# Max-pool and subtract: tiles of six rows in four slots in place of four rows in six

## The chip, the cores and the metric

The kernel runs on one core of one Trainium2 chip. The metric is the device time in microseconds (us) of one execution, as the median of several.

## The reference

```python
B, C, H, W = 8, 64, 256, 256          # float32
x_r = x.reshape(B, C, 32, 8, 32, 8)
pooled = x_r.max(axis=(3, 5))         # maximum of each 8 x 8 window
upsampled = np.repeat(np.repeat(pooled, 8, axis=2), 8, axis=3)
return x - upsampled
```

Every 8 x 8 window of each image has its own maximum subtracted. The input is 134.22 MB, the output as much.

## The kernel before

Eight image lines of one channel, 8 x 256 = 2048 floats or 8 KB, hold 32 whole windows. The kernel calls this a row (`ROW`). There are 16384 rows, or 128 for each of the 128 partitions, and a row in all partitions together is 1.049 MB. A tile is a number of rows per partition: partition p of a tile takes neighbouring rows of DRAM, so that each partition's share is one contiguous piece, 32 KB for a tile of four rows.

The tiles are listed in `sizes`: a first tile of four rows, 30 tiles of four rows (`ROUNDS * SLOTS`), and a last one of four. The first is loaded and stored as two halves of two rows (`HEAD`), the last is loaded whole, and computed and stored in parts of two, one and one row (`TAIL`). The data lie in one SBUF buffer, `ring`, of `SLOTS * SIZE` = 24 rows per partition. Tile i has the slot `(i - 1) % SLOTS`, the first tile the last slot. The maxima lie in `tops`. A tile is computed in place and stored from where it was loaded to.

Nothing is left to a scheduler: each engine has its list of instructions, and semaphores tie them together.

- SyncE issues all loads (L110) in the order of the tiles. Before the load of tile i it waits until the tile that had the slot before is stored (L107, semaphore `stored[slot]`).
- TensorE does no arithmetic. It waits for each load in turn and adds one to `filled` (L117, L120), so that VectorE has one semaphore to wait for.
- VectorE runs two nested loops over `ROUNDS` and `SLOTS` (L139, L140) with the head before and the tail after. For each part it takes one from `filled` (`take`, L75), and calls `pool_and_subtract`: one maximum over the windows of all rows of the part (L81), a wait for it (`reduced`), and one subtraction per row (L93), the last of which adds to `ready`.
- ScalarE waits for `ready` and issues the stores (L129), which add to `stored[slot]` or, at the end, to `final`.

Loads and stores have a DMA queue each (q1 and q10 on the page), over the same 16 DMA engines.

Of the kernel before, what the change touches and what calls it, by code (L numbers as in the profile page):

```python
# [1 line left out]

# [4 lines left out]

F32 = mybir.dt.float32
ROW = 2048


HEAD = [2, 2]
SIZE = 4
ROUNDS = 5
TAIL = [2, 1, 1]
SLOTS = 6


@with_exitstack
def kernel(  # L20
    ctx: ExitStack,
    tc: tile.TileContext,
    x: bass.AP,
    out: bass.AP,
):
    nc = tc.nc
    P = nc.NUM_PARTITIONS
    B, C, H, W = x.shape
    pH = pW = 8
    oW = W // pW  # L30

    x_rows = x.rearrange("b c (oh ph) w -> (b c oh) (ph w)", ph=pH)
    out_rows = out.rearrange("b c (oh ph) w -> (b c oh) (ph w)", ph=pH)
    sizes = [sum(HEAD)] + [SIZE] * (ROUNDS * SLOTS) + [sum(TAIL)]
    assert sum(sizes) * P == x_rows.shape[0] and max(sizes) == SIZE
    starts = [P * sum(sizes[:i]) for i in range(len(sizes))]
    last = len(sizes) - 1

    data = ctx.enter_context(tc.tile_pool(name="data", bufs=1))
    ring = data.tile([P, SLOTS * SIZE * ROW], F32, name="ring")  # L40
    tops = data.tile([P, SLOTS * SIZE * oW], F32, name="tops")
    first = [tc.alloc_semaphore(f"first{i}") for i in range(len(HEAD))]
    loaded = [tc.alloc_semaphore(f"loaded{i}") for i in range(SLOTS)]
    stored = [tc.alloc_semaphore(f"stored{i}") for i in range(SLOTS)]
    final = tc.alloc_semaphore("final")
    filled = tc.alloc_semaphore("filled")
    reduced = tc.alloc_semaphore("reduced")
    ready = tc.alloc_semaphore("ready")

    def slot_of(i):  # L50

        return (i - 1) % SLOTS

    def dram(rows, i):

        n = sizes[i]
        return rows[starts[i] : starts[i] + P * n].rearrange("(p r) d -> p (r d)", r=n)

    def sbuf(i, lo, R):
        at = (slot_of(i) * SIZE + lo) * ROW  # L60
        return ring[:, at : at + R * ROW]

    def top(i, lo, R):
        at = (slot_of(i) * SIZE + lo) * oW
        return tops[:, at : at + R * oW]

    def cuts(parts):
        lo = 0
        for R in parts:
            yield lo, R  # L70
            lo += R

    def take(sem, n):

        nc.vector.wait_ge(sem, n).then_inc(sem, -n)  # L75

    def pool_and_subtract(part, top, R):

        wins = part.rearrange("p (r ph ow pw) -> p r ph ow pw", r=R, ph=pH, ow=oW)
        maxs = top.rearrange("p (r ow) -> p r ow", r=R)  # L80
        nc.vector.tensor_reduce(  # L81
            out=maxs if R > 1 else maxs[:, 0],
            in_=(
                wins.rearrange("p r ph ow pw -> p r ow ph pw")
                if R > 1
                else wins[:, 0].rearrange("p ph ow pw -> p ow ph pw")
            ),
            axis=mybir.AxisListType.XY,
            op=mybir.AluOpType.max,
        ).then_inc(reduced, 1)  # L90
        take(reduced, 1)
        for r in range(R):
            sub = nc.vector.tensor_tensor(  # L93
                out=wins[:, r],
                in0=wins[:, r],
                in1=maxs[:, r].unsqueeze(1).unsqueeze(3).to_broadcast([P, pH, oW, pW]),
                op=mybir.AluOpType.subtract,
            )
        sub.then_inc(ready, 1)

    with tc.tile_critical(no_gpsimd_drain=True):

        landed = [0] * SLOTS
        for i in range(len(sizes)):
            slot = slot_of(i)
            if landed[slot]:
                nc.sync.wait_ge(stored[slot], 16 * landed[slot])  # L107
            for k, (lo, R) in enumerate(cuts(HEAD if i == 0 else [sizes[i]])):
                part = slice(lo * ROW, (lo + R) * ROW)
                nc.sync.dma_start(out=sbuf(i, lo, R), in_=dram(x_rows, i)[:, part]).then_inc(  # L110
                    first[k] if i == 0 else loaded[slot], 16
                )
                landed[slot] += 1


        for k in range(len(HEAD)):
            nc.tensor.wait_ge(first[k], 16).then_inc(filled, 1)  # L117
        for i in range(1, len(sizes)):
            turn = (i - 1) // SLOTS + 1
            nc.tensor.wait_ge(loaded[slot_of(i)], 16 * turn).then_inc(filled, 1)  # L120


        done = n_final = 0
        for i in range(len(sizes)):
            for lo, R in cuts(HEAD if i == 0 else TAIL if i == last else [SIZE]):
                part = slice(lo * ROW, (lo + R) * ROW)
                done += 1
                nc.scalar.wait_ge(ready, done)
                nc.scalar.dma_start(out=dram(out_rows, i)[:, part], in_=sbuf(i, lo, R)).then_inc(  # L129
                    stored[slot_of(i)] if i + SLOTS <= last else final, 16  # L130
                )
                n_final += i + SLOTS > last
        nc.scalar.wait_ge(final, 16 * n_final)


        for lo, R in cuts(HEAD):
            take(filled, 1)
            pool_and_subtract(sbuf(0, lo, R), top(0, lo, R), R)
        with nc.vector.Fori(0, ROUNDS):  # L139
            with nc.vector.Fori(0, SLOTS) as slot:  # L140
                take(filled, 1)
                pool_and_subtract(
                    ring[:, bass.ds(slot * (SIZE * ROW), SIZE * ROW)],
                    tops[:, bass.ds(slot * (SIZE * oW), SIZE * oW)],
                    SIZE,
                )
        take(filled, 1)
        for lo, R in cuts(TAIL):
            pool_and_subtract(sbuf(last, lo, R), top(last, lo, R), R)


# [1 line left out]
_INS = ['x']  # L153
_OUTS = [((8, 64, 256, 256), 'float32')]


# [23 lines left out]
```

## Time and profile before

| | |
|---|---|
| median of 3 runs | 627.47 us (627.42 to 627.5) |
| profiled execution: time | 627.26 us |
| profiled execution: span | 625.5 us |
| VectorE busy | 562.6 us (90%) |
| maximum of a part of 4 rows (L81) | 8.69 us, x30 |
| maximum of a part of 2 rows, 1 row | 4.42 us x3, 2.28 us x2 |
| subtraction of a row (L93) | 2.29 us, x128 |
| loads, stores issued | 33, 35 |
| median from issue to landing, 4 rows | load 62.1 us, store 35.9 us |
| DMA packets | 9792 |

The page divides the span into 40 equal slices and gives for each the busy share of VectorE in tenths, the share of the 16 DMA engines and what they moved. The time from issue to landing includes the time that a transfer stands in its queue behind earlier ones. A wait is named with the line that waits and what it waited for; the line L75 is the wait inside `take`. In the timeline a line has the start, the duration, the engine, the line of code, and in brackets the idle time just before.

### The profile page before, as it was taken

The page shows a single profiled execution, that of the slowest core. Times are in us where ns is not written, and L with a number is a line of the kernel's source. Part 1 is how long each engine was busy: PE and PEld are TensorE (multiplying, and loading weights), DVE is VectorE, ACT ScalarE, POOL GpSimd, SP SyncE. Part 2 cuts the span into 40 slices and gives each one's busy share as a digit, 9 for nine tenths or more (in the row PEclk, how much of TensorE's full clock was granted, in tenths as well). Part 3 has the DMA queues.
Part 4 walks back from the last instruction along what each step waited for, and adds up shares of the span by engine and source line. Part 5 has one row for each costly group of instructions (what it writes and reads, how often), then busy time and mean ns, then how long its engine had stood idle before and what let it go on. Part 6 is the DMA issues. An engine that isn't in the chain of part 4 may idle for free. (4 is left out here: it accounts for less than half of the span.)

```text
span 625.5 us, 613 instructions
## 1 busy us (share of the span) xinstructions
DVE 562.6 (90%) x163; POOL 0.2 (0%) x4
## 2 busy tenths in 40 slices
DVE  4999999998898888988889888898888998888983
POOL 0000000000000000000000000000000000000000
DMA  8999999999999999999999999999999999999998
GB/s 369 402 434 438 436 434 436 434 436 434 434 432 427 425 434 436 436 436 434 436 434 436 434 434 427 430 425 436 436 436 434 436 436 434 434 436 434 425 427 363
DMA packets 9792, 268.44 MB, mean 429 GB/s; under 512 B 1088, under 2 KB 1088, under 8 KB 1088
## 3 DMA queue, kind: packets, MB, share of 16 engines
q1 hardware_dynamic: 4752, 134.22, 49.9%
q10 hardware_dynamic: 5040, 134.22, 49.7%
HBM read 134.22 MB, written 134.22 MB: 429 GB/s over the span
## 5 line engine op out<-in xcount | busy, mean ns | idle before, releaser
L81 DVE TENSOR_REDUCE tops<-ring (+2 forms) x35 | 278.4, 7953 | 48.4 <-DVEq L75 48.4
L93 DVE TENSOR_TENSOR ring<-ring,tops (+1 forms) x128 | 285.0, 2287 | 5.2 <-DVEq L75 0.2
L164 POOL MEMSET const-bfloat16-1.0<- 128x1 bf16 x1 | 0.1, 102 | 0.0
L164 POOL MEMSET const-uint8-127<- 128x1 uint8 x1 | 0.1, 102 | 0.0
L164 POOL MEMSET const-float32-0.0<- 128x1 f32 x1 | 0.1, 99 | 0.2 <-issue 0.2
L164 POOL MEMSET const-float32-1.0<- 128x1 f32 x1 | 0.1, 99 | 0.0
## 6 DMA issues: line engine op xcount, KB each, us to landing
ring<-in_x_dram SPq DMA_DIRECT2D x31, 4096.0 KB, 62.1
out_dram<-ring ACTq DMA_DIRECT2D x30, 4096.0 KB, 35.9
out_dram<-ring ACTq DMA_DIRECT2D x3, 2048.0 KB, 19.3
ring<-in_x_dram SPq DMA_DIRECT2D x2, 2048.0 KB, 9.5
out_dram<-ring ACTq DMA_DIRECT2D x2, 1024.0 KB, 9.2
```

Source lines behind the costliest of these rows:

```text
L81: nc.vector.tensor_reduce(out=maxs if R > 1 else maxs[:, 0], in_=(wins.rearrange("p r ph ow pw -> p r ow ph pw") if R > 1 else wins[:, 0]. ...
L93: sub = nc.vector.tensor_tensor(out=wins[:, r], in0=wins[:, r], in1=maxs[:, r].unsqueeze(1).unsqueeze(3).to_broadcast([P, pH, oW, pW]), op ...
L164: nc = _bacc.Bacc("TRN2", target_bir_lowering=False, num_devices=1)
```

## The change

The 30 tiles of four rows become 20 tiles of six (`SIZE`, `TILES`), and the ring has four slots of six rows in place of six slots of four: the same 24 rows. A partition's share of such a tile is a contiguous piece of 48 KB. The first tile keeps its four rows and its halves (`HEAD` for loads and computing, `HEAD_OUT` for stores, both two and two), and lies in the last slot, of which it fills four of six rows. The last tile keeps its four rows and its parts.

VectorE's two nested loops become one loop over the tiles, with the slot worked out as `i % SLOTS` on each pass. For the head and the last tile, VectorE waits for the load's semaphore itself; TensorE passes on the loads between only. For these parts the wait between the maximum and the subtractions counts up on a semaphore of its own, `pooled`, in place of taking one from `reduced`. The load of tile i again waits for the stores of tile i - `SLOTS`, so tile 4 is the first that waits, for both stores of the head.

```diff
-HEAD = [2, 2]
-SIZE = 4
-ROUNDS = 5
+HEAD, HEAD_OUT = [2, 2], [2, 2]
+SIZE, TILES = 6, 20
 TAIL = [2, 1, 1]
-SLOTS = 6
+SLOTS = 4
...
-    sizes = [sum(HEAD)] + [SIZE] * (ROUNDS * SLOTS) + [sum(TAIL)]
+    sizes = [sum(HEAD)] + [SIZE] * TILES + [sum(TAIL)]
...
+    pooled = tc.alloc_semaphore("pooled")
...
-    def pool_and_subtract(part, top, R):
+    def pool_and_subtract(part, top, R, nth=None):
...
-        ).then_inc(reduced, 1)
-        take(reduced, 1)
+        ).then_inc(reduced if nth is None else pooled, 1)
+        if nth is None:
+            take(reduced, 1)
+        else:
+            nc.vector.wait_ge(pooled, nth)
...
-                landed[slot] += 1
+            landed[slot] += len(HEAD_OUT) if i == 0 else 1
...
-        for k in range(len(HEAD)):
-            nc.tensor.wait_ge(first[k], 16).then_inc(filled, 1)
-        for i in range(1, len(sizes)):
+        for i in range(1, last):
             turn = (i - 1) // SLOTS + 1
             nc.tensor.wait_ge(loaded[slot_of(i)], 16 * turn).then_inc(filled, 1)
...
-            for lo, R in cuts(HEAD if i == 0 else TAIL if i == last else [SIZE]):
+            for lo, R in cuts(HEAD_OUT if i == 0 else TAIL if i == last else [SIZE]):
...
-                done += 1
+                done = [sum(HEAD[: k + 1]) for k in range(len(HEAD))].index(lo + R) + 1 if i == 0 else done + 1
...
-        for lo, R in cuts(HEAD):
+        for k, (lo, R) in enumerate(cuts(HEAD)):
+            nc.vector.wait_ge(first[k], 16)
+            pool_and_subtract(sbuf(0, lo, R), top(0, lo, R), R, k + 1)
+        with nc.vector.Fori(0, TILES) as i:
+            slot = i % SLOTS
             take(filled, 1)
-            pool_and_subtract(sbuf(0, lo, R), top(0, lo, R), R)
-        with nc.vector.Fori(0, ROUNDS):
-            with nc.vector.Fori(0, SLOTS) as slot:
-                take(filled, 1)
-                pool_and_subtract(
-                    ring[:, bass.ds(slot * (SIZE * ROW), SIZE * ROW)],
-                    tops[:, bass.ds(slot * (SIZE * oW), SIZE * oW)],
-                    SIZE,
-                )
-        take(filled, 1)
-        for lo, R in cuts(TAIL):
-            pool_and_subtract(sbuf(last, lo, R), top(last, lo, R), R)
+            pool_and_subtract(
+                ring[:, bass.ds(slot * (SIZE * ROW), SIZE * ROW)],
+                tops[:, bass.ds(slot * (SIZE * oW), SIZE * oW)],
+                SIZE,
+            )
+        nc.vector.wait_ge(loaded[slot_of(last)], 16 * ((last - 1) // SLOTS + 1))
+        for k, (lo, R) in enumerate(cuts(TAIL)):
+            pool_and_subtract(sbuf(last, lo, R), top(last, lo, R), R, len(HEAD) + k + 1)
```

## The prediction

> **What bounds the kernel now.** I read the page's slices first, then its DMA packets and queues, then the waits, then the timeline.
>
> ```profile
> span 625.5 us, 613 instructions
> DVE 562.6 (90%) x163; POOL 0.2 (0%) x4
> ...
> DVE  4999999998898888988889888898888998888983
> ...
> DMA  8999999999999999999999999999999999999998
> GB/s 369 402 434 438 436 434 436 434 436 434 434 432 427 425 434 436 436 436 434 436 434 436 434 434 427 430 425 436 436 436 434 436 436 434 434 436 434 425 427 363
> DMA packets 9792, 268.44 MB, mean 429 GB/s; under 512 B 1088, under 2 KB 1088, under 8 KB 1088
> ...
> q1 hardware_dynamic: 4752, 134.22, 49.9%
> q10 hardware_dynamic: 5040, 134.22, 49.7%
> ```
>
> The reader is to see that the two queues (q1 loads, q10 stores) together occupy the 16 DMA engines for 99.6% of the span, at a flat 434 to 436 GB/s. VectorE is 90% busy, not full. The waits say which way the dependence runs:
>
> ```profile
> DVE tops L81 <- DVEq L75: 48.4, 26, 8.5
> ...
> SPq L110 <- DMA out_dram<-ring: 522.6, 26, 47.2
> ```
>
> VectorE waits 48.4 us in 26 places at its L75 wait, which is the wait for a load; SyncE spends 522.6 us waiting for stores to free a slot. Two lines of the timeline, 22 tiles apart, give the steady period:
>
> ```profile
> 152.70 8.69 DVE L81 TENSOR_REDUCE tops<-ring  x1 [1.64 <-DVEq L75]
> ...
> 578.66 8.69 DVE L81 TENSOR_REDUCE tops<-ring  x1 [1.63 <-DVEq L75]
> ...
> 613.92 2.29 DVE L93 TENSOR_TENSOR ring<-ring,tops 128x2048 f32<-128x2048 f32 x1
> ```
>
> (578.66 - 152.70) / 22 = 19.362 us per tile of four rows, with 1.63 us of idle in it. The last subtraction ends at 616.2, and the last store lands at 624.4: VectorE is done 8 us before the transfers. So the time is DMA bytes and DMA overhead, from the first packet at about 2 us to the end, and nothing else decides unless both queues run empty at once.
>
> [...] The trace has a little more: its packet records show 309, 611 and 1213 ns for packets of 8, 16 and 32 KB, each starting 3.1 to 3.9 ns before the previous one ends, so the true steps are 305.9, 607.1 and 1209.4 ns. Against 301.18 ns per 8 KB at 27.2 GB/s per engine that leaves 4.7 ns for each of the three sizes, and 5.9 ns for the small packet that signals the end. [...] In the trace, load and store packets alternate one to one in the steady part. [...] The pitch here is 32 KB and becomes 48 KB; no run here shows a loss from pitch.
>
> **The change part by part.**
>
> *Transfers.* Bytes are the same: 128 rows of 1.049 MB in and out. A transfer covers 128 partitions, so 8 packets on each of 16 engines, and one small packet each. Before there are 33 loads + 35 stores = 68 transfers: 68 x 128 = 8704 data packets and 68 x 16 = 1088 small ones, as the page counts. After there are 2 + 20 + 1 = 23 loads and 2 + 20 + 3 = 25 stores: 48. Twenty fewer transfers save on each engine 20 x 8 x 4.7 ns + 20 x 5.9 ns = 0.87 us. The period gives the same price another way: 8.389 MB at 435.2 GB/s is 19.275 us, 0.087 us below the measured 19.362; that is 0.043 us for each of the two transfers, and 20 x 0.043 = 0.87 us. This lies on the path in full, since the engines have no idle time. The bounds: the recorded durations taken at face value (1213 = a + 4b, 611 = a + 2b, so a = 9 ns) would give 160 x 9 + 20 x 9 = 1.6 us. From below: if the gain per packet vanishes, 0. I take 0.87, since steps between starts, not durations, make up the time.
>
> *VectorE.* The reduce of 1, 2, 4 rows takes 2.28, 4.42, 8.69 us, about 2.14 per row: 12.96 us for six (estimate). Six subtractions step by 2.205 us: 13.2. With 0.24 us of gaps a tile takes 26.4 us. The DMA period of a six-row tile is 12 x 8 x 0.30118 + 2 x 0.043 = 29.0 us, so VectorE still waits 2.6 us per tile. The added register operation of i % SLOTS and the removed outer loop lie in this idle time: no cost. Without that cover: a branch takes 33 ns and a semaphore wait 21 ns in the trace, so two or three more such per tile, 0.1 us, would be 2 us over 20 tiles. The head and tail waits that go straight to the load's semaphore drop a hop over TensorE's queue; all of VectorE's queue stands behind them, but it waited for the same load before. No cost. SyncE and ScalarE issue 10 fewer transfers each, 0.33 us apiece, beside waits of hundreds of us: nothing.
>
> *Slots, steady.* A slot's round is 4 x 29.0 = 116.0 us (before 6 x 19.36 = 116.2). VectorE holds it 26.4, leaving 89.6 for store and load, which need 29 each while they share: 31 us of spare backlog. Before: 116.2 - 17.7 - 2 x 19.4 = 59.8. Smaller, but not gone. And a dry load queue alone costs nothing, because stores then run at the full rate.
>
> *Start.* The head's two loads are unchanged, so VectorE starts at 8.47 again and the first store goes out at 17.57. By about 19 us some 6.9 rows are in. Tile 1 now needs 10 rows, not 8. Load packets of 48 KB alternate with head stores of 16 KB, so loads get 3/4 of the rate (3.2 us per row): tile 1 lands at about 30 us, VectorE idles 3 to 4 us from 26.4. That idle is paid from its slack. The new wait to watch: SyncE holds tile 4's load (before it was tile 6's) until both head stores landed, and all later loads queue behind it. Those stores have 4 rows at a quarter of the rate, 4 x 2.41 x 4 = 38.5 us, so they land at about 58; the 15 rows then still queued for tiles 1 to 3 last 15 x 3.2 = 48 us, to about 67. Nine us of cover; the engines don't stop.
>
> *End.* The last load (4 rows) lands about 24 us after tile 20's, as its packets alternate with larger store packets ((4 + 6) x 2.41). VectorE spends 26.4 on tile 20, then 18.3 on the tail (597.89 to 616.2 now), so it ends 20.7 us after the last load. Stores left at that load: all of tile 20 and the tail, 10 rows = 24 us, plus what tile 19 has left, some 10 us. So stores end 10 us or more after VectorE, as against 8 now. No cost.
>
> **Sum.** The profiled execution has a span of 625.5 and a time of 627.26; the change takes 0.87: 624.6 and 626.4. The median shown, 627.47, lies 0.21 above it, so I forecast 626.6. That is 0.14% less, inside the 0.2% (1.25 us) that a measurement of this kernel can about tell from no change.
>
> **The rivals.**
> (a) *The forecast*: overhead of 20 transfers goes, nothing else. For it: full engines, identical steps at three packet sizes. With 0.4 us either way for the uneven start of the engines: 626.2 to 627.0. Chance 0.62.
> (b) *Packets of 48 KB run slower*, from the pitch of 48 KB in HBM or a limit of the engine. Place: 40 transfers x 8 = 320 packets per engine, 320 x 1.812 = 580 us of the time. From 2.1 us of loss (0.87 + 1.25), 6.6 ns per packet or 0.37% of the rate, the change ends slower. At 0.5% the time is 626.6 + 2.9 = 629.5. Against it: the step per byte is constant from 8 to 32 KB[...]. For it: the trace has no 48 KB packet, and the point of decision is low. Chance 0.17, a part of it below that point.
> (c) *The transfer isn't one packet per partition.* Cut in 32 + 16 KB: 160 packets more than now per engine instead of 160 fewer, +0.75 - 0.12 = +0.63 us, 628.1, still within 0.2%. Cut in three of 16 KB: 480 more, +2.26 - 0.12 = +2.14 us, 629.6, slower. Against it: packets of 32 KB pass whole. Chance 0.07, nearly half of it slower.
> (d) *The saving is the durations' 9 ns*, 1.6 us, or one of the start's ragged packets goes too: 625.9, faster by 0.25%. Against it: the steps between packet starts. Chance 0.10.
> (e) *Both queues dry with only four slots*, at the first wait for the head stores, where the cover is 9 us: a gap of 2 us gives 628.6, slower. Chance 0.04.
>
> Faster by over 0.2% is (d) and the edge of (a): 0.14. Slower is most of (b), part of (c), and (e): 0.20. Within 0.2%: 0.66. The range 625.7 to 628.7 holds (a), (d), the mild part of (b) and (c), and (e).
>
> **What would show it.** Right: 6144 data packets and 768 small ones; six-row reduces of about 12.96 us; a steady period of 29.0 us per tile with idle of about 2.6 us before the reduce; queues together at 99.5% or more; VectorE done some 10 us before the end; span about 624.6. Wrong: a period of 29.1 or more, which is (b); more than 6912 packets, (c); a slice in the first 80 us well below 400 GB/s other than the first, (e); last subtraction within 4 us of the end, a tail that VectorE sets.

## The result, and the profile after

The changed kernel took 629.48 us as the median of 6 executions (628.4 to 631.29), beside 627.49 us before (627.36 to 627.79). The ratio is 1.0031, with a 95% interval of 1.0016 to 1.0047: slower by 0.3%, where 0.14% faster was forecast. (Ratios, here and below, are to the kernel before, and leave out executions over 1.5% above the fastest of their kernel: one each in experiments 10, 15 and 18.) The second thing to see is the spread: 2.9 us between executions of one program, where the kernel before has 0.4. The profiled execution took 629.67 us with a span of 627.9.

The page of the changed kernel, with the lines that answer to those shown of before (DMA packets count data packets and small ones; a queue's line has packets, MB, and the share of 16 engines' span):

```profile
span 627.9 us, 517 instructions
DVE 560.1 (89%) x153; POOL 0.2 (0%) x4
...
DVE  4699999999998888989898989898898989898991
...
DMA  8999999999999999999999999999999999999996
GB/s 367 434 426 428 432 448 420 435 442 423 438 438 413 442 445 410 442 448 413 442 448 410 442 451 407 445 448 410 445 448 410 445 448 407 448 448 404 458 410 286
DMA packets 6912, 268.44 MB, mean 428 GB/s; under 512 B 768, under 2 KB 768, under 8 KB 768
...
q1 hardware_dynamic: 3312, 134.22, 49.7%
q10 hardware_dynamic: 3600, 134.22, 49.4%
```

The packets are those that were counted: 6144 of data and 768 small ones, so a 48 KB piece does go as one packet. But the two queues fill only 99.1% of a longer span, and the last slice has fallen from 363 to 286 GB/s. (The swing between 404 and 458 GB/s is no larger than counting makes it: sixteen packets of 48 KB that fall into one slice and not its neighbour are 50 GB/s of a slice.) VectorE's waits, and some lines of its timeline:

```profile
DVE tops L81 <- DVEq L75: 43.7, 15, 5.2
```

```profile
221.82 12.95 DVE L81 TENSOR_REDUCE tops<-ring  x1 [3.49 <-DVEq L75]
...
251.74 12.95 DVE L81 TENSOR_REDUCE tops<-ring  x1 [3.51 <-DVEq L75]
...
280.83 12.95 DVE L81 TENSOR_REDUCE tops<-ring  x1 [2.68 <-DVEq L75]
...
542.02 12.95 DVE L81 TENSOR_REDUCE tops<-ring  x1 [2.59 <-DVEq L75]
...
571.02 12.95 DVE L81 TENSOR_REDUCE tops<-ring  x1 [2.59 <-DVEq L75]
...
597.35 4.41 DVE L81 TENSOR_REDUCE tops<-ring 128x64 f32<-128x4096 f32 x1
...
613.04 2.29 DVE L96 TENSOR_TENSOR ring<-ring,tops 128x2048 f32<-128x2048 f32 x1
```

Most tiles keep the period that was worked out (571.02 - 542.02 = 29.00 us, idle 2.59), but not all: from 221.82 to 251.74 it is 29.92, with 3.5 us of idle. A load came about 0.9 us late there, and the time was not won back.

**Where the time went** is in the trace's packet records. A packet starts 3.1 to 3.9 ns, by its size, before the one ahead of it on its engine ends, so the records can be strung into sixteen chains, one for each engine. (Where two ends fall on the same ns, which chain goes on with which packet is open; the figures for single engines are good to some 0.3 us.) A packet's usual duration is the median for its size, and what it takes beyond that is called its excess, or lateness. The usual 48 KB packet takes 1815 ns, a step of 1811.8 after the overlap (the mean of 4868 packets), and the price of the prediction gives 6 x 301.18 + 4.7 = 1811.8: the saving that was forecast is there. The chains, however, don't end together any more:

| | before | after |
|---|---|---|
| end of the chains that had no late packets | 623.2 to 623.6 | 622.8 to 622.9 |
| end of the latest chain | 624.0 | 626.5 |
| excess of packets after 60 us, median engine, us | 0.0 | 0.2 |
| the same, the three worst engines | at most 0.2 | some 3.3, 3.8, 3.8 |

So twelve engines gained, one ended at 623.8, and three lost 3 to 4 us each in 12 to 15 late packets, nearly all of them loads, late by 0.05 to 0.8 us. Each transfer has sixteen small packets, one for each engine (768 for 48 transfers), and its semaphore is waited for at 16, so the slowest engine sets the time. The twelve gained some 0.55 us, not 0.87: at 598.0 us they have no load left and tile 19's stores are done, and they stand for 0.04 to 0.4 us, with late packets of 0.2 in sum at the restart, until the first stores of tile 20 start at 598.3.

### The profile page after: what moved, and what is told of

Read it like the earlier page. It is cut to its first block, busy times and chain, and to the rows that moved or that the text cites. A ratio compares the mean times of both kernels' runs of the same rounds, so it can differ in the third digit from the quotient of the medians.

```text
span 627.9 us, 517 instructions
## 1 busy us (share of the span) xinstructions
DVE 560.1 (89%) x153; POOL 0.2 (0%) x4
```

## The experiments

Four theories at the outset. Theory 1: packets over 32 KB come late. Theory 2: addresses at a pitch of 48 KB do it. Theory 3: four large slots. Theory 4: the code (one loop, other waits). All edits are against the changed kernel, and dots mark lines that are left out; the kernel before, run beside each group of experiments on the same chip, had medians of 627.08 to 627.36 us.

**1. The code with the old sizes.**

```diff
-SIZE, TILES = 6, 20
-SLOTS = 4
+SIZE, TILES = 4, 30
+SLOTS = 6
```

> The changed code (one loop, direct waits for head and tail) with the old sizes: tiles of four rows, six slots. Theory 1, the size of the load packets (48 KB) makes some of them late: none here, so 627.5 us and runs within 0.3 us of each other. Theory 2, the addresses (pieces at a pitch of 48 KB, so that two DMA engines meet in HBM): also 627.5. Theory 3, four large slots: also 627.5. Theory 4, the code itself: about 629.5 and runs that spread over 2 us or more.

Measured: 627.98 us (627.05 to 628.49), ratio 1.0005 (0.9997 to 1.0014). The code makes no difference that can be measured; theory 4 falls.

**2. Six-row tiles at another pitch.** Two tiles share a block of twelve rows per partition in DRAM.

```diff
+BLOCK = 2
...
+        if 0 < i < last:
+            b, j = divmod(i - 1, BLOCK)
+            lo, n = P * (sizes[0] + b * BLOCK * SIZE), BLOCK * SIZE
+            whole = rows[lo : lo + P * n].rearrange("(p r) d -> p (r d)", r=n)
+            return whole[:, j * SIZE * ROW : (j + 1) * SIZE * ROW]
```

> The changed kernel, but two tiles share a block of twelve rows per partition in DRAM: packets stay 48 KB, the pitch between partitions becomes 96 KB. Theory 1 (packet size): as the changed kernel, 629.5 us with a wide spread. Theory 2 (addresses): different meetings, so a different time; if pieces 96 KB apart keep clear of each other, 626.6. Theory 3 (slots): 629.5.

Measured: 630.34 us, 22 executions from 626.01 to 635.21; ratio 1.0043 (1.0026 to 1.006). As wide as theory 1 has it. Four executions lie at 626.01 to 626.28, somewhat under the 626.5 (627.36 - 0.87) of 48 KB without late packets. That suggests that the lateness comes and goes; these four have no trace. In the profiled execution (635.21 us) one engine alone lost 9.2 us after 85 us, the next worst 0.65. The end shows what that costs. Stretches of its trace near the end (length, VectorE busy, POOL busy, clock, DMA share, GB/s):

```profile
594.00:598.00 4.00, 4.00 (x3) 0.00 (x0) 1.00 0.92 397
598.00:602.00 4.00, 4.00 (x3) 0.00 (x0) 1.00 0.06 25
602.00:606.00 4.00, 4.00 (x2) 0.00 (x0) 1.00 0.95 406
```

In the trace of the changed kernel the middle one reads

```profile
598.00:602.00 4.00, 3.97 (x2) 0.00 (x0) 1.00 1.12 479
```

Two lines of experiment 2's timeline:

```profile
576.70 12.95 DVE L87 TENSOR_REDUCE tops<-ring  x1 [2.74 <-DVEq L81]
...
603.03 4.41 DVE L87 TENSOR_REDUCE tops<-ring 128x64 f32<-128x4096 f32 x1
```

Tile 20 starts at 576.70 in place of 571.02, since its load waited for the one slow engine. By 598 the other fifteen have nothing left, and they stand still for 5.1 to 6.0 us, until tile 20, which VectorE has done at about 603, can be stored.

**3. Four-row tiles at a pitch of 96 KB**, the same block of twelve rows cut into three tiles.

```diff
-SIZE, TILES = 6, 20
+SIZE, TILES = 4, 30
...
-SLOTS = 4
+BLOCK = 3
+SLOTS = 6
...
```

> Tiles of four rows in six slots, with the changed code, but three tiles share a block of twelve rows in DRAM: packets of 32 KB at a pitch of 96 KB in place of 32 KB. Theory 1 (packet size) and theory 3 (slots): 627.5 us, narrow. Theory 2 (addresses, a pitch that isn't a power of two): late load packets appear, 628.5 to 631 and wide.

Measured: 627.84 us (626.98 to 628.34), no late packet after the start. The pitch of 96 KB, no power of two, makes no 32 KB packet late.

**4. Loads in halves**, stores whole.

```diff
+LOAD = [3, 3]
...
-            for k, (lo, R) in enumerate(cuts(HEAD if i == 0 else [sizes[i]])):
+            for k, (lo, R) in enumerate(cuts(HEAD if i == 0 else LOAD if i < last else [sizes[i]])):
...
```

> The changed kernel, but each six-row tile is loaded by two transfers of three rows each: load packets of 24 KB at the same pitch of 48 KB, same slots, same code. 20 more transfers cost 0.87 us. Theory 1 (packet size): the late load packets go, 626.6 + 0.9 = 627.5 us, runs within 0.5 us. Theory 2 (addresses): they stay, 629.5 + 0.9 = 630.4 and a wide spread. Theory 3 (slots): as theory 2, 630.4.

Measured: 660.22 us. All theories missed. Packets are late on every engine, 10 to 30 us each, loads and stores alike. A second loss lies at the end: packets of both queues take turns, so by their sizes loads of 24 KB against stores of 48 get a third of the bytes (an estimate; in the changed kernel, loads of 48 KB beside the head's stores of 16 had 0.76 of them from 26 to 44 us, where turns give 0.75), the stores run out, and from 615 to 630 us the engines wait for VectorE (257 and 293 GB/s in the slices from 607 to 640 us, where the slices between the first and those have 375 to 447). The new question was whether unequal sizes are a cause of their own (theory 5).

**5. Tiles of five rows**, packets of 40 KB.

```diff
-SIZE, TILES = 6, 20
+SIZE, TILES = 5, 24
```

> The changed kernel with tiles of five rows: 24 tiles in four slots of five, packets of 40 KB. 12 transfers fewer than before save 0.5 us: 626.9 if no packet is late. Theory 1 (packets over 32 KB become late once an engine runs out of step with the others): 627 to 629 and a spread of 1 us or more. Theory 2 (addresses that aren't multiples of 32 KB): as the changed kernel, about 629 and a spread of 3 us. Theory 3 (four slots): about 629.

Measured: 626.70 us (13 executions, 626.62 to 626.82), ratio 0.999 (0.9982 to 0.9998). By its median this is the fastest version here, 0.1% faster than the kernel before, with the smallest spread. Its page:

```profile
span 624.9 us, 557 instructions
...
DMA packets 8064, 268.44 MB, mean 430 GB/s; under 512 B 896, under 2 KB 896, under 8 KB 896
...
q1 hardware_dynamic: 3888, 134.22, 49.9%
q10 hardware_dynamic: 4176, 134.22, 49.7%
```

Four slots, a pitch of 40 KB and 12 transfers fewer: 12 x 0.0436 = 0.52 us should be saved, and 0.62 was. The queues are back at 99.6%. No load packet is late after the start. Theories 2 and 3 lose, and so does theory 1 in its plain form, since 40 KB is over 32.

**6. The same tiles in pieces of 16 KB**: each partition's six rows are three pieces in DRAM, with the transfers and slots as they were.

```diff
+            whole = rows[lo : lo + P * 2 * SIZE].rearrange("(p k j r) d -> p j k (r d)", k=SIZE // 2, j=2, r=2)
+            return whole[:, j]
...
```

> The changed kernel with the same tiles, slots and number of transfers, but each partition's six rows are three separate pieces of two rows in DRAM (two tiles share twelve rows): packets of 16 KB for loads and stores. 480 packets more per engine than before cost 2.3 us, 20 transfers fewer give 0.1. Theory 1 (packet size): no late packets, 629.5 us with a spread under 1 us. Theory 2 (addresses at odd multiples of 16 KB): late packets on top, 631 or more. Theory 3 (four large slots): late packets, 631 or more and wide.

Measured: 629.23 us (629.05 to 629.61). The price of a packet, 4.7 ns, gave 629.5. No late packets, at odd multiples of 16 KB and with four slots of six rows: theories 2 and 3 are out.

**7. Loads and stores in halves**, 24 KB in both queues.

```diff
+LOAD = [3, 3]
+STORE = [3, 3]
...
```

> The changed kernel with every six-row tile loaded and stored by two transfers of three rows: packets of 24 KB in both queues, at the pitch of 48 KB. 20 transfers more than before: 0.9 us. Theory 1 (packet size): 628.3, spread under 1 us. Theory 2 (addresses): 630 or more and wide. Theory 5, that only unequal packet sizes in the two queues put engines out of step (24 KB against 48 KB in the run with halved loads alone): 628.3, as the sizes are equal again.

Measured: 628.26 us (627.6 to 628.41). The forecast by count was 628.3. No late packets, so the 24 KB of experiment 4 weren't at fault, but their being unequal to the stores'.

**8. Four rows, four slots.**

```diff
-SIZE, TILES = 6, 20
+SIZE, TILES = 4, 30
```

> The changed code with tiles of four rows and only four slots (16 rows in the ring): packets of 32 KB at the old addresses. Theory 1 (packet size) and theory 2 (addresses): 627.4 to 628, as with six slots. Theory 3 (four slots leave too little in the queues): 629 or more.

Measured: 628.00 us (627.75 to 628.3), no late packets. Four slots don't make packets late. The ratio, 1.001 (1.0003 to 1.0017), leaves some 0.7 us that no theory here accounts for.

**The engines' step.** The chains show one thing more. Each engine takes a load and a store packet in turn. The small packet at a transfer's end counts as a turn too (in the traces of before, after, five rows and halves no two packets of one queue follow each other on an engine between 100 and 560 us; in the first two these are 6848 and 4569 packets). In the run of five rows all sixteen engines take their turns together: at 300 us the next load starts 2.47 to 2.77 us later on every one, the next store 0.96 to 1.25. In the changed kernel the store of tile 1 reaches a store queue that has had no data to move since 57.7 us. Two engines start it at 61.2 and 61.3 us, the other fourteen, which had just begun another load, at 62.7 to 62.9. These two are then out of step: at 103 us, say, they store while the others load. They are the two that lost 3.8 us; the third late engine started with the fourteen. So theory 6: being out of step is the cause, whatever the size. A measure of it is the number of engines that do the rarer of the two kinds at a time, as a mean over 85 to 590 us: 8 would be half and half. It is 0.8 in the run of five rows, 2.0 before, and 2.6 in the changed kernel. The theory was tested by putting engines out of step at the start, with small loads that run on eight engines only (the page of experiment 9 counts eight small packets for each such load, not sixteen).

**9 to 11. Eight engines put out of step**, with packets of 32, 40 and 48 KB (SHIFT is 4, 5 and 6).

```diff
...
+        for m in range(SHIFT):
+            nc.scalar.dma_start(out=extra[8 * m : 8 * m + 8], in_=x_rows[8 * m : 8 * m + 8]).then_inc(final, 16)
```

> Tiles of four rows in six slots with the changed code, and at the start four more small loads of 8 partitions, 64 KB each, into a buffer that nothing reads: they run on eight of the sixteen engines and put these four packets of 8 KB, 1.2 us, behind the others, about half a period of load and store. Theory 1 (long packets are late where engines are out of step): 32 KB isn't long enough, so only the 1.2 us: 628.6, spread under 1 us. Theory 6, that being out of step is enough by itself: 630 or more, wide.

> Tiles of five rows in four slots, with five such small loads at the start: eight engines run 1.5 us behind the others. If packets of 40 KB stay on time even out of step: 626.7 + 1.5 = 628.2, narrow. If 40 KB is long enough to be late and only the engines' step kept the run of five rows clean: 629 or more and a spread of 1 us or more.

> The changed kernel with six such small loads at the start: eight engines run 1.8 us behind the others. Theory 1: nearly every engine now meets others out of step and many load packets are late: 632 or more. If the step of the engines has no part in it: 629.5 + 1.8 = 631.3 with the old spread, and late packets on three or four engines as before.

Measured: 630.74 us (630.24 to 631.08), 634.1 (630.2 to 640.34) and 642.22 (641.4 to 644.22). At 32 KB no load packet is late after the start; what was over the expected 628.6 is for the most part a start that is 1.6 us longer. This run is a weak test, though: eight engines were behind by one whole packet, so they mostly still loaded while the others loaded (measure 2.0). The stronger case came unasked: in experiment 3 the measure is 5.0, and no packet of 32 KB is late there. At 40 KB the shift raises the measure from 0.8 to 4.5 and turns the clean kernel into one with 66 late loads and executions over 9 us apart. At 48 KB (4.8) there are 239 late loads. So the step alone does nothing at 32 KB, and 40 KB alone does nothing in step: theory 6 falls, and what is left is the two together. These runs count late packets in one trace each; their times also hold the longer start.

**12. Unequal sizes, small packets**: four-row tiles, loads of 16 KB against stores of 32.

```diff
-SIZE, TILES = 6, 20
+SIZE, TILES = 4, 30
...
-SLOTS = 4
+LOAD = [2, 2]
+SLOTS = 6
...
```

> Tiles of four rows in six slots, each loaded by two transfers of two rows: load packets of 16 KB against store packets of 32 KB, the same ratio as 24 KB against 48 KB in the run with halved loads. 30 transfers more cost 1.3 us: 628.7, and where the loads' smaller share of the engines leaves the stores without work at the end, up to 9 us on top. Theory 1 (packet size): no late packets after the start, whatever the time. Theory 5 (unequal sizes in the two queues make packets late): late packets on all engines, as there.

Measured: 643.0 us. Late packets on all engines, some 10 us each. Theory 5 holds: unequal packets in the two queues are a cause of their own, with no packet over 32 KB too.

**13. 24 KB, out of step** (experiment 7 with SHIFT = 6).

> The run with halves (packets of 24 KB in both queues, 48 KB pitch) with the six small loads at the start. Packets of equal size up to 32 KB are on time even out of step: 628.3 + 1.8 for the shift + 1.5 for the longer start seen with it = 631.6, no late load packets after the start. If any step between engines is enough at this pitch: late load packets and 635 or more.

Measured: 633.78 us (633.66 to 633.91), no late load packet. The measure of step is 5.0. The 2.2 us over the expected are mostly the start: packets before 60 us are late by 4.7 us per engine in sum, where experiment 7 has about 1.4, and 1.5 of the difference had been allowed for.

**14. Loads alone, out of step.** The loop over the tiles on VectorE and the tiles' stores are left out, so the output isn't computed. The load of tile i waits for the load that had its slot before.

> The changed kernel with the six small loads at the start that put eight engines out of step, but the 20 six-row tiles are only loaded: their computing and their stores are left out, so the loads run alone between head and tail. 134.22 MB at 435 GB/s is 308 us, with start and tail about 335. If loads are late because other engines read at the same time: late load packets here too, 3 us per engine and more. If it takes another engine's stores: none after the start.

Measured: 353.31 us in one execution; the head's stores (9.6 us) and a longer start had been left out of the 335. Not one of the 1984 load packets of 48 KB from 85 us to 40 us before the end is late. So loads of 48 KB that run alone came on time, in this one trace; it takes stores beside them.

**15. A longer head**, to keep the store queue filled.

```diff
-HEAD, HEAD_OUT = [2, 2], [2, 2]
-TAIL = [2, 1, 1]
+HEAD, HEAD_OUT = [2, 2, 2], [2, 2, 2]
+TAIL = [1, 1]
```

> The changed kernel with a head of six rows in three parts of two, and a last tile of two rows in parts of one: the same 20 tiles of six, the same packets of 48 KB. Six head rows keep the store queue filled until about 75 us, while tile 1 is ready to be stored at about 62: the stores don't stop and start again, so all engines keep one step. Theory 7 (48 KB packets are late only on engines that fell out of step when the stores of tile 1 started on an empty store queue): no late packets, 626.2 us, spread under 0.5 us. If 48 KB packets are late by their size alone: 629 or more and a spread of 3 us as in the changed kernel.

Measured: 631.18 us (628.0 to 638.93), 77 late loads. Not what was expected, but not an answer either: at 30 us several engines were already out of step. They had parted at the first store of all, and the time of unequal packets (16 KB stores against 48 KB loads) had been made longer.

**16 and 17. A pause**, in which both queues run empty and start again; beside it the changed kernel once more.

The first lines hold back the load of tile 4 until the store of tile 1 is issued, the last two hold that store back until tile 3 has landed.

```diff
+            if i == SLOTS:
+                nc.sync.wait_ge(go, 1)
...
+                if i == 2:
+                    nc.scalar.wait_ge(ready, done - 1).then_inc(go, 1)
                 nc.scalar.wait_ge(ready, done)
+                if i == 1:
+                    nc.scalar.wait_ge(loaded[slot_of(SLOTS - 1)], 16)
```

> The changed kernel with one pause: the store of tile 1 waits until tile 3 has landed, and the load of tile 4 is issued just after that store, so both queues are empty for some 3 us near 67 us and all engines start together, store first. Everything else, packets of 48 KB, slots and tiles, is as in the changed kernel. If 48 KB packets are late only where engines are out of step: no late packets after the pause, 626.2 + 3 = about 629.2, spread under 0.7 us. If they are late by their size alone: late packets as in the changed kernel, 632 or more and a spread of 3 us.

> The changed kernel once more, on the same chip as the run with the pause. Either theory: 629.5 us, spread of 2 to 3 us, and the engines with late load packets are those that are out of step with the rest.

Measured: 630.47 us (630.09 to 632.12) and 630.23 (629.74 to 630.39). The pause didn't bring the engines together: at 75 us there are two groups. It settles nothing on 48 KB in step. The changed kernel, seen a second time, has 31 late loads, again on a few engines: some 3.8 and 3.0 us on two, 1.0 and 0.7 on two more. One of the four, which lost 3.8, had started the store of tile 1 ahead of the rest (61.6 us, the others from 62.9); that the late engines would be those out of step came true for it alone.

**18. The first store held back**, so that the head's stores last until tile 1 is there.

```diff
                 nc.scalar.wait_ge(ready, done)
+                if i == 0 and lo == 0:
+                    nc.scalar.wait_ge(pooled, 2)
```

> The changed kernel with one more wait: the first store of the head goes out only when the second half's maximum is done (21.6 us, not 17.3). In the changed kernel the head's stores end at 57.2 to 57.7 us, and the store of tile 1 reaches the empty queue about 61.2, where two engines start it at 61.2 and 61.3 and fourteen at 62.7 to 62.9: this splits the engines. With the wait the head's stores last until about 61.7, the queue isn't empty when tile 1 arrives, and all engines start it in step. If 48 KB packets are late only where engines are out of step: no late load packets after 85 us, 626.2 us, spread under 0.5. If their size alone makes them late: late packets as in the changed kernel, 629.5 and a spread of 2 to 3 us.

Measured: 627.98 us, 17 executions from 625.97 to 636.86; ratio 1.0019 (0.9999 to 1.0039). No new split arises at tile 1, as meant, but in the profiled execution five engines had parted at the first store, at 25.5 us. After 60 us those five lost 0.7, 1.6, 1.8, 3.4 and 3.8 us; of the eleven others one lost 0.9 and the rest 0.1 or less. Seven executions lie at 625.97 to 626.97, about the forecast's 626.2.

**The counts in one table**: load packets over 50 ns late, from 85 us to 590 (or to 40 us before the end), counted from the packet records of each profiled execution.

| kernel | packets, load and store, KB | mean engines out of step | late loads |
|---|---|---|---|
| before | 32, 32 | 2.0 | 0 of 3298 |
| old sizes in the changed code | 32, 32 | 2.6 | 0 of 3302 |
| four rows, four slots | 32, 32 | 1.9 | 0 of 3297 |
| four rows, pitch 96 KB | 32, 32 | 5.0 | 0 of 3311 |
| four rows, shifted | 32, 32 | 2.0 | 0 of 3325 |
| pieces of 16 KB | 16, 16 | 3.5 | 0 of 6446 |
| halves | 24, 24 | 2.1 | 0 of 4351 |
| halves, shifted | 24, 24 | 5.0 | 0 of 4365 |
| five rows | 40, 40 | 0.8 | 0 of 2629 |
| five rows, shifted | 40, 40 | 4.5 | 66 of 2666 |
| changed kernel | 48, 48 | 2.6 | 45 of 2236 |
| changed kernel, again | 48, 48 | 2.4 | 31 of 2239 |
| six rows, pitch 96 KB | 48, 48 | 1.3 | 34 of 2238 |
| first store held back | 48, 48 | 3.6 | 34 of 2228 |
| with a pause | 48, 48 | 3.4 | 36 of 2230 |
| longer head | 48, 48 | 4.6 | 77 of 2253 |
| six rows, shifted | 48, 48 | 4.8 | 239 of 2224 |
| loads alone, shifted | 48, none | | 0 of 1984 |
| four rows, loads halved | 16, 32 | 3.4 | 349 of 6506 |
| six rows, loads halved | 24, 48 | 3.1 | 339 of 4298 |

**Where in a tile the late loads lie** is in the same records, and no experiment was made on it. When a transfer's small packet takes a turn of the store queue, the engine runs two loads in a row. In the changed kernel 288 of the loads, one in eight, come right after the small packet of a store, and 26 of the 45 late ones are among them; 22 of 31 in experiment 17, about half of the 34 in experiment 2, 27 of 34 in experiment 18, but only 9 of 36 with the pause. Nor do late loads come evenly: of the 45, 32 start before 283 us, nine between 300 and 560, though three engines run 1.4 us or more behind the others from about 300 us on. So being out of step isn't all that it takes at 48 KB.

## Why the prediction was wrong

- **The price of a transfer was right.** The usual step of a 48 KB packet is 1811.8 ns, and 1811.8 follow from the price. The rates in it are those of the trace of before: the steps of 305.9, 607.1 and 1209.4 ns for 8, 16 and 32 KB lie 301.2 ns apart per 8 KB, which is 27.2 GB/s on an engine and 435.2 on sixteen, and leave 4.7 ns for each packet. The same 4.7 ns per packet and 5.9 ns per signal gave 629.5, 628.3 and 626.9 for experiments 6, 7 and 5, which measured 629.23, 628.26 and 626.70. The sum of all recorded durations, divided by 16, fell from 623.38 to 622.47 us; that this is 0.91, near the forecast's 0.87, is chance. The durations contain the overlaps, so without late packets it would have fallen by some 1.6, and late packets, those of the start counted in, gave back 0.7.
- **VectorE, the start and the slots were right.** The reduce of six rows took 12.95 us against 12.96, the period is 29.00 against 29.0, the idle time 2.59 against 2.6; the data of the head's stores ended at 57.2 to 57.7 us and their signals, a turn later, at 59.1 to 59.5, against 58. VectorE began tile 1 at 31.27, after 5.2 us of idle, not 3 to 4; it cost nothing. The start's rates were right too: beside the head's stores the loads had 0.76 of the bytes from 26 to 44 us and took 3.3 us per row, where 3/4 and 3.2 were worked out. A queue alone kept the engines full, as was taken: before, loads alone moved 430 GB/s (3 to 17 us) and stores alone 425 (598.5 to 622.5 us), with the engines busy for 100 and 99%. The direct waits and the slot by register cost nothing that can be measured (experiment 1: ratio 1.0005); VectorE's own branches at its loop's line took 50 to 63 ns, not the 33 of the prediction, which is a branch of ScalarE's queue.
- **The step that failed** is "this lies on the path in full, since the engines have no idle time". It treats sixteen engines as one. The end is set by the slowest of them, and with 48 KB packets some come late: 3.8 us on the worst engine against 0.87 gained, so the latest chain ended at 626.5 in place of 624.0. The sum lacks that term.
- **Rival (b) was nearest and was put too low**, at 0.17. "The step per byte is constant from 8 to 32 KB" says nothing of 48, and the point of decision, 0.37% of the rate, was known to be low; what holds an engine at 27.2 GB/s no run shows. Its picture was wrong too: the usual step of a 48 KB packet is 1811.8 ns, as worked out. It is not all packets that are slower, but 45 of 2236 loads, each by 0.05 to 0.8 us. That its example, a rate lower by 0.5%, came to 629.5, as was measured, is luck. It lay outside the range that was given, which should have reached 630.
- **The end** came out much as worked out. On the latest engine the last load landed 24.8 us after tile 20's (594.96 and 570.18), and VectorE ended 20.4 us after it, at 615.3. On most engines tile 19 had 9 us of stores left at their last load (589.0 to 598.0). The latest transfer ended over 11 us after VectorE, but the twelve punctual engines only 7.5, not 10. What the working left out is that tile 20's stores must be handed over before those of tile 19 run out. VectorE began tile 20 after the late engines' load at 570.18, where the first engine had its share at 564.78, and the hand-over came 0.04 to 0.4 us too late for the twelve. In the trace of experiment 2 the same thin cover turned one engine's delay into 5.1 to 6.0 idle us for the rest.
- Chances: slower was given 0.20, and the interval of the ratio, 1.0016 to 1.0047, holds 1.002. By its median it is slower by more than that.

**What is shown and what isn't.** Shown by intervention: with the same tiles and slots, cutting packets of 48 KB to 16 or 24 KB in both queues makes the late loads go. Equal packets of 16 to 32 KB are on time with a mean of up to 5 engines of 16 out of step, 40 KB packets are on time in step and late out of step, unequal packets are late at 16 against 32 KB, and loads of 48 KB without stores are on time. Each count is of one profiled execution. For 48 KB the tie to the step is by observation: much of the lateness sits on engines out of step (one of one in experiment 2, five of the six in experiment 18, two of four in the changed kernel, one of four in experiment 17). The crowding of late loads at the ends of store transfers is a rival, or a part of the cause, that no run has tested. No profiled execution had all engines in step with 48 KB packets, so whether they would then be on time stays open; the fastest executions, 625.97 and 626.01, have about the time of that case, but no trace. Where the delay arises, and why 32 KB is spared, no run here tells.

## What to carry to other kernels

Where transfers bound a kernel, work out the saving from larger ones by the small price of a packet and a signal (here 4.7 and 5.9 ns), but then look at the slowest engine, and at the spread of the executions, not at the mean. Keep the packets of the load queue and the store queue of equal size (unequal ones made 643.0 and 660.22 us here, of 627), and treat a packet size that the trace hasn't shown as unknown in both directions; here packets of 40 KB gained 0.62 us, with a spread of 0.2 us over 13 executions, but experiment 10 shows that they too are late once engines are out of step; up to 32 KB no trace has late loads after the start where the two queues' packets are equal. A single late engine cost most where the queues were about to run empty (5.1 to 6.0 us of the fifteen others in experiment 2), so leave cover at the end.

## What the runs showed of the hardware

- Unequal packets in two queues that share the engines came late: 16 against 32 KB made 643.0 us where 628.7, and up to 9 us on top for the end, were worked out (experiment 12), with packets late by some 10 us in sum on every engine.
- About the time at which stores began beside running loads, packets were late on every engine for a few us: loads by about 0.8 us per engine at the first store of the kernel before (19 to 23 us), by 0.2 at that of the changed kernel (19 to 23 us) and 0.6 at its second (27.1 us), and at the restart of experiment 16 by about 1.5 us, stores too.
- The small packet that signals the end of a transfer used up a turn: with it counted, no two of 4569 packets in a row on an engine of the changed kernel were of one queue. In step, this shows as two data packets of the other queue in a row at each transfer's end: in the run of five rows no store runs on any engine for 2.7 us once in every 24 us.
